# A convolution's eighth chunk ahead of the taps of the sixth and seventh, with all its taps on VectorE and GpSimd

## The chip, the cores and the metric

The kernel runs on one core of a Trainium2 chip. The metric is the device time of one execution in microseconds, as the median of several runs. TensorE, VectorE (DVE in the profile), ScalarE (ACT), GpSimd (POOL) and the DMA queues work side by side, each through its own instructions in order.

## What is computed

The program is a decoder trunk of two layers on 512 tokens of width 1024, in float32: a Conformer convolution module, then differential attention, each followed by a SwiGLU block and a gated embedding. The change lies in the convolution module of the first layer:

```python
a = x @ w_pw1 + b_pw1
u = a[..., :D_MODEL] * jax.nn.sigmoid(a[..., D_MODEL:])
u = lax.conv_general_dilated(u, dw_w[:, None, :], window_strides=(1,),
        padding=[(CONV_WIDTH - 1, 0)], ..., feature_group_count=D_MODEL) + dw_b
u = jax.nn.silu(layer_norm(u, ln_g, ln_b))
return u @ w_pw2 + b_pw2
```

The convolution is depthwise: each of the 1024 features has its own 31 taps over the tokens. The layer norm needs, for every token, the sum and the sum of squares over all 1024 features.

## The kernel before

Features lie on the 128 partitions and tokens along the free axis, so the 1024 features are eight chunks of 128x512, numbered 0 to 7 in the code; "the eighth chunk" is number 7. Large products run as three matmuls on high and low parts (`mm3`, L159 to L161); a weight tile is loaded by SyncE, rounded to its high part on ScalarE (L152) and its low part is taken on VectorE (L154).

The loop over `c` (L480 to L527) makes one chunk per turn. Two halves of 24 matmuls each (`half`) give the gate `pg` and the value `pa`; VectorE scales them (L503, L509), ScalarE takes the sigmoid (L504), and VectorE puts the chunk together (L521, or L513 for a phased chunk). The taps of chunk c-1 are in turn c.

There are two ways to do a chunk's 31 taps. The chunks 1, 3, 5 and 6 are *phased*: the chunk goes through DRAM into another layout (`phased_in`, buffers `pi` and `C1`), TensorE does all its taps as 36 matmuls with prepared matrices (`phased_taps`, L387; matrices loaded by SyncE at L367, L373 and L377 into the buffers `D0` to `D5` and `C5`), and the result goes back through DRAM: ScalarE copies it out of PSUM (L395) and starts the store (L397), SyncE loads it in four pieces (L400), and VectorE adds bias and shift (L405, called the shift below). The other chunks share their taps between engines. For chunk 7 TensorE does 8 taps with diagonal matrices (L343), ScalarE forms 7 products (L422, L425) that GpSimd adds (L426), and VectorE does 16 taps as one multiply-and-add each (L435, L438). VectorE then adds the three parts (L442, L444).

`moments` (L456) squares a finished chunk on ScalarE (L466) and adds square and chunk to running sums, on GpSimd for most chunks and on VectorE for chunk 6 (L471, L473). The last chunk is not added: TensorE sums over the partitions with matmuls by ones (L192), once for the running sums and once for the last chunk and its square. From these follow mean and variance (L565 to L567, L254, a power on GpSimd at L256), a row of factors (L575, L578), the normalised chunks (L589 to L594), and the second product (`linear`).

Between the taps and these sums stand five *factors*: `project` does a small product of the gated embedding ahead of time, six matmuls in a PSUM tile "mm", and ScalarE copies it out (L305). They are ordered behind the last tap on TensorE.

PSUM tiles come from pools: four "mm", two "sc" and two "tp" buffers, each one bank. A tile gets its buffer where the scheduler places its first use. The kernel's order on each engine is made by a scheduler that goes by estimated times and by the waits between instructions; `tc.issue_after(x)` keeps an instruction behind x.

Of the kernel before, what the change touches and what calls it, by code (L numbers as in the profile page):

```python
# [14 lines left out]
AF = mybir.ActivationFunctionType  # L15
ALU = mybir.AluOpType
# [4 lines left out]
P = 128  # L21
S = 512
# [4 lines left out]
KW = 31  # L27
# [20 lines left out]

SHIFT = 1
WARM = 9  # L50
ALONE = (7,)
CUTS = 2


PE_TAPS = (0, 0, 0, 0, 0, 0, 0, 8)
POOL_TAPS = (10, 0, 11, 0, 11, 0, 0, 7)


PHASED = (1, 3, 5, 6)
# [25 lines left out]
def trunk(ctx, tc, xT, pT, wts, diag, dww, vec, rel, onehot, lamv, out):  # L85
# [29 lines left out]
    def col(name, i=0):  # L115
        a, _ = VEC[name]
        return vt[:, a + i : a + i + 1]
# [181 lines left out]
    def project(ph, m, w, o, step=lambda: None):  # L299

        acc = mm()
        for k in range(2):
            last_product[0] = mm3(acc, wpart(w, 2 * (m % 4) + k), ph[k], k == 0, k == 1)
            step()
        last_copy[0] = A.copy(o, acc)  # L305
        return o

    last_copy = [None]
    y = []
    PAD = KW - 1  # L310
    ups = {}
    accs = {}
    last_tap = [None]
    last_out = [None]
    last_shift = [None]
    last_v_tap = [None]
    last_sum = [None]
    rb = None

# [6 lines left out]
    def wt(c, j):  # L326
        return dwt[:, c * KW + j : c * KW + j + 1]
# [64 lines left out]
    def phased_out(c):  # L392

        o = big()
        last_out[0] = A.copy(o, accs[c])  # L395
        d = dram.tile([P, S], F32, tag=f"po{c}", name=f"po{c}")
        nc.scalar.dma_start(d, o)  # L397
        both_ = sb([P, 2, S], f"B{c}", 1)
        for g in range(NPH):
            nc.sync.dma_start(  # L400
                both_[g * FG : (g + 1) * FG, 1].rearrange("p (r n) -> p r n", r=NPH),
                bass.AP(d.tensor, d.offset + g * P, [[S, FG], [FG * S, NPH], [1, P]]),
            )
        tok = "p (n r) -> p n r"
        last_shift[0] = V.scalar_tensor_tensor(  # L405
            both_[:, 0].rearrange(tok, r=NPH), both_[:, 1].rearrange("p (r n) -> p n r", r=NPH), col("dw_b", c),
            shrow.rearrange(tok, r=NPH), ALU.add, ALU.add,
        )
        y.append(both_[:, 0])

    def other_taps(c):
        if c in PHASED:
            return phased_out(c)
        up, acc = ups[c], accs[c]
        alone = c in ALONE
        tap = lambda j: up[:, j : j + S]
        a, b = PE_TAPS[c], PE_TAPS[c] + POOL_TAPS[c]
        pacc = wk()
        for j in range(a, b):
            if j == a:  # L420
                with tc.issue_after(last_out[0].ins) if alone else nullcontext():
                    A.activation(pacc, tap(j), AF.Identity, scale=wt(c, j), bias=col("dw_b", c))  # L422
            else:
                pr = sb([P, S], f"C{2 + j % 2}", 2)
                A.activation(pr, tap(j), AF.Copy, scale=wt(c, j))  # L425
                G.tensor_tensor(pacc, pacc, pr, ALU.add)  # L426
        yc = sb([P, 2, S], f"B{c}", 1)
        if c == 0:
            sums["acc"] = yc[:, 1]
        yc = yc[:, 0]  # L430
        sum_ = sc() if alone else acc
        if c == 0:
            V.tensor_scalar(sum_, tap(b), wt(c, b), None, ALU.mult)
        else:
            V.scalar_tensor_tensor(sum_, tap(b), wt(c, b), shrow, ALU.mult, ALU.add)  # L435
        for j in range(b + 1, KW):
            with tc.issue_after(last_shift[0].ins) if alone and j == KW - 4 else nullcontext():
                last_v_tap[0] = V.scalar_tensor_tensor(sum_, tap(j), wt(c, j), sum_, ALU.mult, ALU.add)  # L438
        if alone:
            moments(NC - 2)  # L440
        with tc.issue_after(last_sum[0].ins) if alone else nullcontext():
            V.tensor_tensor(yc, sum_, pacc, ALU.add)  # L442
        if alone:
            last_add[0] = V.tensor_tensor(yc, acc, yc, ALU.add)  # L444
        y.append(yc)

# [4 lines left out]
    macc = sb([P, S], "acc", 1)  # L451
    last_moment = [None]
    last_add = [None]
    last_factor = [None]

    def moments(c):  # L456
        if c == 0:
            t = tp()
            T.matmul(t, ones, y[0], start=True, stop=True)
            A.activation(shrow, t, AF.Copy, scale=-1.0 / P)  # L460
            V.scalar_tensor_tensor(y[0], t, -1.0 / P, y[0], ALU.mult, ALU.add)
            A.activation(sums["acc"], y[0], AF.Square)
            return
        sq = sums["sq"] = wk()
        with tc.issue_after(last_factor[0].ins) if c > NC - 3 else nullcontext():
            A.activation(sq, y[c], AF.Square)  # L466
        if c == NC - 1:
            return
        eng, at = (V, tc.issue_after(last_v_tap[0].ins)) if c == NC - 2 else (G, nullcontext())
        with at:  # L470
            last_sum[0] = eng.tensor_tensor(sums["acc"], sums["acc"], sq, ALU.add)  # L471
            if c > 1:
                eng.tensor_tensor(macc, y[1] if c == 2 else macc, y[c], ALU.add)  # L473

    def add_moments(a, b, first, last):

# [3 lines left out]
    for c in range(NC):  # L480
        wa, wg = pairs[c]
        if c == 0:
            pg = half(wg)
            pa = half(wa)
            norm.dg = diagonal(norm.columns_of_chunks())
            rb = norm.rows()
        if c + 1 < NC:
            pairs.append((weight(), weight())[::-1])
            pair_loads.append(loaded[0])
        if c == 0:  # L490
            dwt = sb([P, NC * KW], "C4", 2)
            nc.sync.dma_start(dwt, dww)
        if c == 1:
            ph = pfeatures(0, [(sb([P, S], t, 2, F32R), sb([P, S], t, 2, F32R)) for t in ("wth", "wtl")])
        if c > 0:
            pg = half(wg)
            if c - 1 not in PHASED:
                pe_taps(c - 1)
            pa = half(wa)
            if c - 1 in PHASED:  # L500
                pe_taps(c - 1)
        tg, ta = big(), big()
        V.tensor_tensor(tg, pg, rb, ALU.mult)  # L503
        gated = A.activation(tg, tg, AF.Sigmoid, bias=col("b_pw1", 8 + c))  # L504
        if c == NC - 1:

            with tc.issue_after(gated.ins):
                A.activation(sb([P, 8], "lam", 1), vt[:, :8], AF.Silu)
        V.tensor_tensor(ta, pa, rb, ALU.mult)  # L509
        if c in PHASED:  # L510
            up = big()
            phases, tok = "p (r n) -> p n r", "p (n r) -> p n r"
            V.scalar_tensor_tensor(  # L513
                up.rearrange(phases, r=NPH), ta.rearrange(tok, r=NPH), col("b_pw1", c),
                tg.rearrange(tok, r=NPH), ALU.add, ALU.mult,
            )
            phased_in(c, up)
        else:
            up = ups[c] = sb([P, S + PAD], "C0", 2)
            G.memset(up[:, :PAD], 0.0)  # L520
            V.scalar_tensor_tensor(up[:, PAD:], ta, col("b_pw1", c), tg, ALU.add, ALU.mult)  # L521
        if c > 0:
            other_taps(c - 1)
        if c == 1:
            moments(0)
        elif c > 3:
            moments(c - 3)  # L527
# [16 lines left out]
    moments(NC - 3)  # L544
    pe_taps(NC - 1)
    for m in range(5):
        factor(last_tap)
        if m == 1:
            last_factor[0] = last_copy[0]
    other_taps(NC - 1)  # L550
    moments(NC - 1)

    sums["cols"], sums["mean"], sums["mcols"] = tp(), tp(), sc()
    with tc.issue_after(last_product[0].ins):
        add_moments(macc, sums["acc"], True, False)
        add_moments(y[NC - 1], sums["sq"], False, True)
    factor(last_moment)

    with tc.issue_after(last_product[0].ins):
        T.matmul(sums["mean"], ones, macc, start=True, stop=False)  # L560
        last_product[0] = T.matmul(sums["mean"], ones, y[NC - 1], start=False, stop=True)


    vs = sb([P, P // 2], "v8", 2)[:, :8]
# [61 lines left out]
        V.scalar_tensor_tensor(h[m], acc, col("b_pw2", m), h[m], ALU.add, ALU.add)  # L626
        norm.chunk(m)

    linear(NC, z, add_conv, 3, split={0: (last_add[0], None), 1: (last_add[0], None), 2: (layer_v, None), 3: third}, home=("C5", 2))


    def ffn(norm, after):
# [510 lines left out]
```

## Time and profile before

| | us |
|---|---|
| median of 3 runs | 1277.39 (1276.99 to 1279.48) |
| profiled execution, its own time | 1276.96 |
| its span in the profile | 1275.0 |
| TensorE busy | 1264.7 |
| VectorE busy | 707.7 |
| ScalarE busy | 524.5 |
| GpSimd busy | 246.1 |

The span runs from the first instruction on any engine to the last; the execution's own time holds 1.96 us more around it. In the timeline a row has its start, its length, the engine, the line, the operation with its tiles, and behind brackets how long the engine had been idle and what ended that. Matmul rows overlap each other by some 0.16 us, so the pace of matmuls is read from start to start. The convolution's last part lies between 110 and 160 us of the span.

### The profile page before, as it was taken

What the parts mean: (1) busy time and instruction counts of PE and PEld (TensorE: products, weight loads), DVE (VectorE), ACT (ScalarE), POOL (GpSimd) and SP (SyncE); (2) the same over time, 40 slices, a digit from 0 to 9 for tenths busy, and PEclk for the clock granted to TensorE, in tenths of its full rate; (3) what the DMA queues carried; (4) which work ended last, traced back from release to release, by engine and by line L of the source; (5) the groups of instructions that cost most, each with busy time, mean ns of one, the idle gap of its engine ahead of it and who ended that gap; (6) DMA issues with size and microseconds to landing.
All of it is one profiled execution on the core that took longest, in us unless ns stands there. A gap on an engine that the chain in (4) does not pass through costs nothing.

```text
span 1275.0 us, 15493 instructions
## 1 busy us (share of the span) xinstructions
PE 1264.7 (99%) x5960; PEld 1050.7 (82%) x5960; DVE 707.7 (56%) x1042; ACT 524.5 (41%) x876; POOL 246.1 (19%) x223
## 2 busy tenths in 40 slices
PE   9999999999999999999999999999999999999998
PEld 8888788888888888888888888888888888888887
DVE  4997865543344434366777876646443444334545
ACT  5653454332222223254666877744231222123332
POOL 1654432000000000042346635141000000000120
PEclk9999999999999999999999999999999999999999
DMA  7655213333332222233432330133223333222231
GB/s 269 199 181 174 92 58 125 88 96 98 99 99 99 94 90 98 75 127 124 139 110 82 106 99 26 65 134 100 95 89 97 99 99 99 97 87 91 89 116 66
DMA packets 49142, 136.17 MB, mean 107 GB/s; under 512 B 5635, under 2 KB 10243, under 8 KB 49068
## 3 DMA queue, kind: packets, MB, share of 16 engines
q1 hardware_dynamic: 46944, 131.74, 31.6%
q10 hardware_dynamic: 2124, 3.43, 0.8%
q8 instruction: 47, 0.77, 0.2%
q14 instruction: 27, 0.22, 0.1%
HBM read 128.84 MB, written 6.31 MB: 106 GB/s over the span
## 4 chain that ended last, share of the span: by engine, by line
PE 87%; DVE 5%; DMA 3%; POOL 2%; issue 2%; ACT 1%; SPq 0%; POOLq 0%; DVEq 0%; ACTq 0%
PE mm L159 27%; PE mm L160 27%; PE mm L161 27%; DVE sc L438 2%; POOL wk L426 2%; PE mm L871 1%; DVE wlo L154 1%; DMA wraw<-in_wts 1%; DMA po<-big 1%; PE sc L839 1%; PE sc L838 1%; PE tp L858 1%; PE tp L792 1%; ACT whi L152 0%; ACT A L199 0%
## 5 line engine op out<-in xcount | busy, mean ns | idle before, releaser
L152 ACT CAST whi<-wraw 128x1024 fp32r<-128x1024 f32 (+2 forms) x209 | 213.2, 1026 | 551.3 <-PE mm L161 364.1
L159 PE MATMUL mm<-A,wlo 128*128 128x512 f32 (+1 forms) x1080 | 421.3, 390 | 0.6 <-ACT A L199 0.5
L160 PE MATMUL mm<-A,whi 128*128 128x512 f32 (+1 forms) x1080 | 419.3, 388 | 0.0
L161 PE MATMUL mm<-A,whi 128*128 128x512 f32 (+1 forms) x1080 | 416.0, 389 | 0.0
L154 DVE TENSOR_TENSOR wlo<-wraw,whi 128x1024 fp32r<-128x1024 f32 (+2 forms) x205 | 253.2, 1239 | 88.2 <-ACT whi L152 88.2
L159 PEld LDWEIGHTS mm<-A,wlo 128*128 128x128 f32 x1080 | 203.0, 188 | 43.7 <-issue 1.2
L160 PEld LDWEIGHTS mm<-A,whi 128*128 128x128 f32 x1080 | 203.0, 188 | 42.3 <-issue 1.2
L161 PEld LDWEIGHTS mm<-A,whi 128*128 128x128 f32 x1080 | 202.7, 188 | 41.4 <-issue 0.5
L223 POOL TENSOR_TENSOR acc<-acc,wk 128x512 f32<-128x512 f32 x35 | 57.9, 1653 | 772.3 <-issue 660.0
L159 PE MATMUL mm<-B,wlo 128*128 128x512 f32 x352 | 137.8, 391 | 0.0
L160 PE MATMUL mm<-B,whi 128*128 128x512 f32 x352 | 137.5, 390 | 0.0
L161 PE MATMUL mm<-B,whi 128*128 128x512 f32 x352 | 137.4, 390 | 0.0
L658 DVE TENSOR_TENSOR h<-mm,h 128x512 f32<-128x512 f32 x48 | 33.0, 691 | 123.3 <-PE mm L161 123.2
L650 DVE TENSOR_TENSOR big<-mm,rb 128x512 f32<-128x512 f32 x44 | 30.4, 691 | 126.4 <-PE mm L161 126.4
L648 DVE TENSOR_TENSOR big<-mm,rb 128x512 f32<-128x512 f32 x44 | 30.4, 691 | 99.9 <-PE mm L161 93.0
L161 PEld LDWEIGHTS mm<-B,whi 128*128 128x128 f32 x352 | 66.1, 188 | 14.5
L159 PEld LDWEIGHTS mm<-B,wlo 128*128 128x128 f32 x352 | 66.1, 188 | 14.3
L160 PEld LDWEIGHTS mm<-B,whi 128*128 128x128 f32 x352 | 66.1, 188 | 14.2
L159 PE MATMUL mm<-whi,A 128*128 128x512 f32 x192 | 76.5, 401 | 0.0
L161 PE MATMUL mm<-wlo,A 128*128 128x512 f32 x192 | 75.3, 398 | 0.0
L160 PE MATMUL mm<-whi,A 128*128 128x512 f32 x192 | 75.1, 393 | 0.0
L426 POOL TENSOR_TENSOR wk<-wk,C 128x512 f32<-128x512 f32 x35 | 51.9, 1483 | 24.4 <-ACT C L425 19.5
(225 smaller groups left out, 1378.0 us busy)
## 6 DMA issues: line engine op xcount, KB each, us to landing
wraw<-in_wts SPq DMA_DIRECT2D x193, 512.0 KB, 3.5
wraw<-in_wts SPq DMA_DIRECT2D x16, 384.0 KB, 2.9
D<-in_diag SPq DMA_DIRECT2D x22, 256.0 KB, 4.1
C<-in_diag SPq DMA_DIRECT2D x16, 256.0 KB, 5.0
h<-in_xT SPq DMA_DIRECT2D x8, 256.0 KB, 5.4
rest<-h SPq DMA_DIRECT2D x8, 256.0 KB, 3.0
bias<-scr ACTq DMA_DIRECT2D x8, 256.0 KB, 3.3
h<-rest SPq DMA_DIRECT2D x8, 256.0 KB, 2.7
```

Source lines behind the costliest of these rows:

```text
L152: A.copy(hi[:, cut], raw[:, cut])
L154: eng.tensor_tensor(lo[:, cut], raw[:, cut], f(hi[:, cut]), ALU.subtract)
L159: T.matmul(acc, al, bh, start=first, stop=False)
L160: T.matmul(acc, ah, bh, start=False, stop=False)
L161: return T.matmul(acc, ah, bl, start=False, stop=last)
L223: self.last = self.eng.tensor_tensor(self.acc, self.acc, sq, ALU.add)
L426: G.tensor_tensor(pacc, pacc, pr, ALU.add)
L438: last_v_tap[0] = V.scalar_tensor_tensor(sum_, tap(j), wt(c, j), sum_, ALU.mult, ALU.add)
L648: V.tensor_tensor(tg, pg, rb, ALU.mult)
L650: V.tensor_tensor(tu, pu, rb, ALU.mult)
L658: V.tensor_tensor(h[m], acc, h[m], ALU.add)
L792: T.transpose(t[:, i * P : (i + 1) * P], q[:, i * P : (i + 1) * P], ident)
```

## The change

Chunk 7's taps leave TensorE: GpSimd (with ScalarE) takes 10 of the 31, VectorE 21. Its accumulator on VectorE is the tile `accs[7]`, which `pe_taps` takes from the "mm" pool and which TensorE used before. The turn c = 6 does no taps, and in turn 7 both halves of chunk 7 come ahead of the taps of chunks 5 and 6. `phased_out` is split: storing and loading stay in it, the shift is `phased_shift`. The shift of chunk 5 is put between chunk 7's taps, behind tap 21. The running sums take in chunk 7 (on VectorE), and the chunk that is left for last is chunk 6.

```diff
-PE_TAPS = (0, 0, 0, 0, 0, 0, 0, 8)
-POOL_TAPS = (10, 0, 11, 0, 11, 0, 0, 7)
+PE_TAPS = (0, 0, 0, 0, 0, 0, 0, 0)
+POOL_TAPS = (10, 0, 11, 0, 11, 0, 0, 10)
...
-        sum_ = sc() if alone else acc
         if c == 0:
-            V.tensor_scalar(sum_, tap(b), wt(c, b), None, ALU.mult)
+            V.tensor_scalar(acc, tap(b), wt(c, b), None, ALU.mult)
         else:
-            V.scalar_tensor_tensor(sum_, tap(b), wt(c, b), shrow, ALU.mult, ALU.add)
+            V.scalar_tensor_tensor(acc, tap(b), wt(c, b), shrow, ALU.mult, ALU.add)
         for j in range(b + 1, KW):
-            with tc.issue_after(last_shift[0].ins) if alone and j == KW - 4 else nullcontext():
-                last_v_tap[0] = V.scalar_tensor_tensor(sum_, tap(j), wt(c, j), sum_, ALU.mult, ALU.add)
-        if alone:
-            moments(NC - 2)
-        with tc.issue_after(last_sum[0].ins) if alone else nullcontext():
-            V.tensor_tensor(yc, sum_, pacc, ALU.add)
-        if alone:
-            last_add[0] = V.tensor_tensor(yc, acc, yc, ALU.add)
-        y.append(yc)
+            r = V.scalar_tensor_tensor(acc, tap(j), wt(c, j), acc, ALU.mult, ALU.add)
+            if between and j == KW - 10:
+                with tc.issue_after(r.ins):
+                    between()
+        last_add[0] = V.tensor_tensor(yc, acc, pacc, ALU.add)
...
             pg = half(wg)
-            if c - 1 not in PHASED:
-                pe_taps(c - 1)
             pa = half(wa)
-            if c - 1 in PHASED:
-                pe_taps(c - 1)
+            for k in ([c - 1], [], [c - 2, c - 1])[max(0, c - NC + 3)]:
+                pe_taps(k)
...
-    moments(NC - 3)
+    copies = []
+    phased_out(NC - 3)
+    phased_out(NC - 2)
     pe_taps(NC - 1)
     for m in range(5):
         factor(last_tap)
-        if m == 1:
-            last_factor[0] = last_copy[0]
-    other_taps(NC - 1)
+    other_taps(NC - 1, lambda: phased_shift(NC - 3))
+    moments(NC - 3)
     moments(NC - 1)
+    with tc.issue_after(last_sum[0].ins):
+        last_add[0] = phased_shift(NC - 2)
+    moments(NC - 2)
...
-        add_moments(y[NC - 1], sums["sq"], False, True)
+        add_moments(y[NC - 2], sums["sq"], False, True)
```

In `moments` the squares of chunks 6 and 7 are ordered behind the copies of the fifth and fourth factor, and the square of chunk 6 is the one that is not added to the running sum. The third weight of `linear` is rounded behind that square.

More of the change, by code (lines that the diff above doesn't have):

```diff
@@ L50 @@
 WARM = 9
-ALONE = (7,)
 CUTS = 2
-PE_TAPS = (0, 0, 0, 0, 0, 0, 0, 8)
-POOL_TAPS = (10, 0, 11, 0, 11, 0, 0, 7)
+PE_TAPS = (0, 0, 0, 0, 0, 0, 0, 0)
+POOL_TAPS = (10, 0, 11, 0, 11, 0, 0, 10)
 PHASED = (1, 3, 5, 6)
@@ L308, in trunk @@
     last_copy = [None]
-    y = []
+    y = [None] * NC
     PAD = KW - 1
@@ L313, in trunk @@
     last_tap = [None]
-    last_out = [None]
-    last_shift = [None]
-    last_v_tap = [None]
     last_sum = [None]
@@ L394, in phased_out @@
         o = big()
-        last_out[0] = A.copy(o, accs[c])
+        A.copy(o, accs[c])
         d = dram.tile([P, S], F32, tag=f"po{c}", name=f"po{c}")
         nc.scalar.dma_start(d, o)
-        both_ = sb([P, 2, S], f"B{c}", 1)
+        both_ = y[c] = sb([P, 2, S], f"B{c}", 1)
         for g in range(NPH):
@@ L403, in phased_out, with phased_shift @@
             )
-        tok = "p (n r) -> p n r"
-        last_shift[0] = V.scalar_tensor_tensor(
+    def phased_shift(c):
+        both_, tok = y[c], "p (n r) -> p n r"
+        y[c] = both_[:, 0]
+        return V.scalar_tensor_tensor(
             both_[:, 0].rearrange(tok, r=NPH), both_[:, 1].rearrange("p (r n) -> p n r", r=NPH), col("dw_b", c),
@@ L408, in phased_out, with other_taps @@
         )
[L409 to L413, printed above, removed]
+    def other_taps(c, between=None):
         up, acc = ups[c], accs[c]
-        alone = c in ALONE
         tap = lambda j: up[:, j : j + S]
-        a, b = PE_TAPS[c], PE_TAPS[c] + POOL_TAPS[c]
+        b = POOL_TAPS[c]
         pacc = wk()
[L419 to L422, printed above, removed]
+        for j in range(b):
+            if j == 0:
+                A.activation(pacc, tap(j), AF.Identity, scale=wt(c, j), bias=col("dw_b", c))
             else:
@@ L429, in other_taps @@
             sums["acc"] = yc[:, 1]
-        yc = yc[:, 0]
-        sum_ = sc() if alone else acc
+        yc = y[c] = yc[:, 0]
         if c == 0:
-            V.tensor_scalar(sum_, tap(b), wt(c, b), None, ALU.mult)
+            V.tensor_scalar(acc, tap(b), wt(c, b), None, ALU.mult)
         else:
-            V.scalar_tensor_tensor(sum_, tap(b), wt(c, b), shrow, ALU.mult, ALU.add)
+            V.scalar_tensor_tensor(acc, tap(b), wt(c, b), shrow, ALU.mult, ALU.add)
         for j in range(b + 1, KW):
-            with tc.issue_after(last_shift[0].ins) if alone and j == KW - 4 else nullcontext():
-                last_v_tap[0] = V.scalar_tensor_tensor(sum_, tap(j), wt(c, j), sum_, ALU.mult, ALU.add)
-        if alone:
-            moments(NC - 2)
-        with tc.issue_after(last_sum[0].ins) if alone else nullcontext():
-            V.tensor_tensor(yc, sum_, pacc, ALU.add)
-        if alone:
-            last_add[0] = V.tensor_tensor(yc, acc, yc, ALU.add)
-        y.append(yc)
+            r = V.scalar_tensor_tensor(acc, tap(j), wt(c, j), acc, ALU.mult, ALU.add)
[3 more added lines that the diff above has]
+        last_add[0] = V.tensor_tensor(yc, acc, pacc, ALU.add)
     shrow = sb([P, S], "shrow", 1)
@@ L453, in trunk @@
     last_add = [None]
-    last_factor = [None]
+    last_square = [None]
     def moments(c):
@@ L464, in moments @@
         sq = sums["sq"] = wk()
-        with tc.issue_after(last_factor[0].ins) if c > NC - 3 else nullcontext():
-            A.activation(sq, y[c], AF.Square)
-        if c == NC - 1:
+        with tc.issue_after(copies[10 - c].ins) if c >= NC - 2 else nullcontext():
+            last_square[0] = A.activation(sq, y[c], AF.Square)
+        if c == NC - 2:
             return
-        eng, at = (V, tc.issue_after(last_v_tap[0].ins)) if c == NC - 2 else (G, nullcontext())
+        eng, at = (V, tc.issue_after(last_add[0].ins)) if c == NC - 1 else (G, nullcontext())
         with at:
-            last_sum[0] = eng.tensor_tensor(sums["acc"], sums["acc"], sq, ALU.add)
             if c > 1:
                 eng.tensor_tensor(macc, y[1] if c == 2 else macc, y[c], ALU.add)
+            last_sum[0] = eng.tensor_tensor(sums["acc"], sums["acc"], sq, ALU.add)
     def add_moments(a, b, first, last):
@@ L521, in trunk @@
             V.scalar_tensor_tensor(up[:, PAD:], ta, col("b_pw1", c), tg, ALU.add, ALU.mult)
-        if c > 0:
-            other_taps(c - 1)
+        if 0 < c < NC - 2:
+            (phased_out if c - 1 in PHASED else other_taps)(c - 1)
+            if c - 1 in PHASED:
+                phased_shift(c - 1)
         if c == 1:
@@ L542, in factor @@
             pp.append(project(ph, m, pw[m // 4], o))
-    moments(NC - 3)
+        copies.append(last_copy[0])
+    copies = []
+    phased_out(NC - 3)
+    phased_out(NC - 2)
     pe_taps(NC - 1)
@@ L560, in trunk @@
         T.matmul(sums["mean"], ones, macc, start=True, stop=False)
-        last_product[0] = T.matmul(sums["mean"], ones, y[NC - 1], start=False, stop=True)
+        last_product[0] = T.matmul(sums["mean"], ones, y[NC - 2], start=False, stop=True)
     vs = sb([P, P // 2], "v8", 2)[:, :8]
@@ L627, in add_conv @@
         norm.chunk(m)
-    linear(NC, z, add_conv, 3, split={0: (last_add[0], None), 1: (last_add[0], None), 2: (layer_v, None), 3: third}, home=("C5", 2))
+    linear(NC, z, add_conv, 3, split={0: (last_add[0], None), 1: (last_add[0], None), 2: (layer_v, last_square[0]), 3: third}, home=("C5", 2))
     def ffn(norm, after):
```

## The prediction, made before the changed kernel was run

> **What bounds the kernel now.** I read the page first, then TensorE by stretches, then VectorE's and ScalarE's rows in time order. The page:
>
> ```profile
> PE 1264.7 (99%) x5960; PEld 1050.7 (82%) x5960; DVE 707.7 (56%) x1042; ACT 524.5 (41%) x876; POOL 246.1 (19%) x223
> ```
>
> TensorE is busy 99% of the span, so an edit gains only what it takes off TensorE, and loses what it makes TensorE wait. The stretch that changes, cut where one kind of matmul gives way to the next (columns: stretch, its length, PE busy and count, granted clock, DMA share, GB/s):
>
> ```profile
> 111.40:119.84 8.44, 8.05 (x73) 1.00 0.55 188
> 119.84:127.65 7.81, 7.81 (x37) 1.00 0.90 296
> 127.65:135.69 8.04, 8.04 (x74) 1.00 0.41 112
> 135.69:142.16 6.47, 6.47 (x19) 1.00 0.40 141
> 142.16:149.39 7.23, 7.23 (x33) 1.00 0.00 1
> 149.39:153.30 3.91, 3.91 (x34) 1.00 0.00 0
> ```
>
> In order: the sixth chunk's taps (after 0.39 us without work), the rest of the eighth chunk's projection, the seventh's taps, the eighth's eight taps on TensorE, five factors, the layer norm's column sums. Beside them VectorE (start, length, what):
>
> ```profile
> 115.84 3.92 DVE L438 SCALAR_TENSOR_TENSOR sc<-C,C,sc 128x512 f32<-128x512 f32 x5
> ...
> 122.41 0.69 DVE L503 TENSOR_TENSOR big<-mm,rb 128x512 f32<-128x512 f32 x1 [1.86 <-PE mm L161]
> 126.33 0.15 DVE L730 TENSOR_SCALAR lam<-vec 128x1 f32<-128x1 f32 x1 [3.23 <-ACT lam L508]
> ...
> 131.00 1.12 DVE L405 SCALAR_TENSOR_TENSOR B<-B,vec,shrow 128x512 f32<-128x512 f32 x1 [4.45 <-DMA B<-po]
> 132.04 0.68 DVE L509 TENSOR_TENSOR big<-mm,rb 128x512 f32<-128x512 f32 x1
> 132.75 1.34 DVE L521 SCALAR_TENSOR_TENSOR C<-big,vec,big 128x512 f32<-128x512 f32 x1
> 134.13 1.66 DVE L435 SCALAR_TENSOR_TENSOR sc<-C,C,shrow 128x512 f32<-128x512 f32 x1
> 135.82 8.67 DVE L438 SCALAR_TENSOR_TENSOR sc<-C,C,sc 128x512 f32<-128x512 f32 x11
> 144.40 1.16 DVE L405 SCALAR_TENSOR_TENSOR B<-B,vec,shrow 128x512 f32<-128x512 f32 x1
> 145.49 3.12 DVE L438 SCALAR_TENSOR_TENSOR sc<-C,C,sc 128x512 f32<-128x512 f32 x4
> 148.51 0.68 DVE L473 TENSOR_TENSOR acc<-acc,B 128x512 f32<-128x512 f32 x1
> 149.11 0.68 DVE L471 TENSOR_TENSOR B<-B,wk 128x512 f32<-128x512 f32 x1
> 149.71 0.68 DVE L442 TENSOR_TENSOR B<-sc,wk 128x512 f32<-128x512 f32 x1
> 150.50 0.69 DVE L444 TENSOR_TENSOR B<-mm,B 128x512 f32<-128x512 f32 x1
> 151.11 2.35 DVE L154 TENSOR_TENSOR wlo<-wraw,whi 128x1024 fp32r<-128x1024 f32 x2
> ...
> 153.84 0.16 DVE L567 SCALAR_TENSOR_TENSOR v<-tp,v 128x4 f32<-128x4 f32 x1
> ```
>
> The eighth chunk's output is complete at 150.50 + 0.69 = 151.19, and TensorE's last sums start with it: today the two engines arrive together. From here on the layer norm is a chain, so whatever moves the last chunk's output moves the rest of the kernel as one block. Two numbers are compared below: the last output (151.19) and L567, which waits for the last column sums (153.84).
>
> **The change, part by part.** *TensorE.* The eighth chunk's projection comes ahead of the sixth's taps, its eight taps leave. From 111.40: projection 7.81, taps 8.05 (its projection is in SBUF by then, and the 0.39 us wait for VectorE goes), taps 8.04: the factors start at 135.30, not 142.16, 6.86 us earlier (6.47 and 0.39). The seventh chunk's tap matrices reuse the sixth's buffers, whose last reads now end only as the seventh's begin; each still has about 4 us from release to use, so I count 0, and up to 1 us late.
>
> *The accumulator: the term that decides.* VectorE now sums the eighth chunk's taps in the tile that TensorE used, one of the four "mm" tiles in PSUM, where before it summed in an "sc" tile of its own. In the program as built from the changed kernel, that tile is given the bank of the **second factor's product**: the first tap on VectorE (the new L428) waits for ScalarE's copy of that factor (L304, today L305), and VectorE's later work is queued in order behind it. So the projection was moved forward for taps that cannot start until the factors run. ScalarE's copies and its square of the last output:
>
> ```profile
> 144.14 0.59 ACT L305 COPY D<-mm 128x512 f32<-128x512 f32 x1 [2.81 <-PE mm L161]
> 145.50 0.59 ACT L305 COPY D<-mm 128x512 f32<-128x512 f32 x1 [0.78 <-PE mm L161]
> ...
> 151.23 0.63 ACT L466 ACTIVATE wk<-B 128x512 f32<-128x512 f32 x1 [1.47 <-DVE B L444]
> ```
>
> The second copy ends at 146.09, 3.93 us after the factors' start; so at 139.2 afterwards. Today the first tap starts at 134.13.
>
> *VectorE's chain from 139.2.* One tap more ahead of the shift, and nine in place of four behind it: 21 taps for 16. What the first tap costs depends on GpSimd:
>
> ```profile
> 73.23 0.74 DVE L435 SCALAR_TENSOR_TENSOR sc<-C,C,shrow 128x512 f32<-128x512 f32 x1
> 137.95 8.72 POOL L426 TENSOR_TENSOR wk<-wk,C 128x512 f32<-128x512 f32 x6 [2.72 <-ACT wk L422]
> ```
>
> It took 1.66 at 134.13 and 0.74 at 73.23; the bounds are these two. GpSimd's nine adds (six today, 1.45 each) take 13.1 us from about 126, once the eighth chunk and its first products are there, and end at about 139, as the tap starts: I take 0.77 with the step to the next. [...]
>
> Then: 0.77 → 139.97; eleven taps as at 135.82, to the next start 8.58 → 148.55; the sixth chunk's shift, 1.09 to the next start → 149.64; nine taps of 0.79 (8.67 for eleven) = 7.1 → 156.75; one add with GpSimd's part, 0.79 as from 149.71 to 150.50 (today two adds, the second is gone) → 157.54; the sum of outputs at 157.54, done at 158.2; the sum of squares waits for ScalarE's square of the eighth chunk (157.5 + 0.63) → 158.15; the seventh's shift 0.60 later and 1.12 long → **159.87**. Its data landed long before (today 144.40 at the latest, for taps that end 0.39 later). Against 151.19 this is **+8.7 us**. TensorE's 6.86 us are hidden entirely: they bring the factors' end to 142.53, and TensorE then waits until 158.2. ScalarE's three more products, GpSimd's three more adds and two diagonal loads of 256 KB less lie beside that wait and cost nothing.
>
> *TensorE after a wait of 15.7 us.* No row shows one: its longest idle here is 1.19 us. The nearest are the kernel's first matmuls, which also follow idleness, against equal ones in mid-kernel:
>
> ```profile
> 1.51 4.21 PE L134 MATMUL tp<-ones,ident 128*128 128x128 f32 x18 [1.51 <-POOL ident masks.py:199]
> 5.37 0.77 PE L159 MATMUL mm<-A,wlo 128*128 128x512 f32 x1
> 5.95 0.60 PE L160 MATMUL mm<-A,whi 128*128 128x512 f32 x1
> 6.37 1.07 PE L192 MATMUL tp<-ones,wk 128*128 128x128 f32 x8
> ...
> 149.39 1.05 PE L192 MATMUL sc<-ones,acc 128*128 128x128 f32 x8
> ```
>
> Eighteen passes took 4.21 us, 0.23 each; eight take 0.89 to the next group at 150.28 or about 0.11 each; full pace came near 6.0, 4.5 us after the first. The granted clock reads 1.00 for both, so it does not show this. Bounds: nothing is lost, or all four groups of column sums run at 1.87 instead of about 0.95. Nearest row, same kind of matmul: half pace for 4.5 us. Sums of outputs from 158.25 to 160.1, of squares to 162.0, the seventh chunk's (ready at 159.9) to 163.3 with the pace rising at 162.75, its squares to 164.3; L567's successor at about 164.4, **+10.5 us** against 153.84. At full pace throughout, the four end at 162.0, but VectorE's two weight splits (2.27) last to 162.14 and the two short steps ahead of it 0.46: 162.65, +8.8. At half pace throughout, 165.7 and 165.9: +12.0. [...]
>
> **Sum.** The profiled execution took 1276.96 us (span 1275.0 and 1.96 around it); the median of the three runs, 1277.39, is 0.43 above. 1276.96 + 8.7 for the last output + 1.8 for the cold restart = **1287.5 us**. Past L567 the order is the same, with the same distances.
>
> **Rivals.**
> *A, the wait does not bind* (the bank is free in time, and the change does what it says). The tap could start when the eighth chunk is ready: three of the five taps at 115.84 done by 118.2, then its gate multiplication; the small constants ended 4.1 us after that one's start (122.41 to 126.5), so 122.3, then one add, 0.6, 0.68 and up to 1.34 → 124.9. Then the sixth chunk's shift binds. Its taps end at 127.3, and from taps' end to shift today took 8.7 us (135.69 to 144.40) and 11.2 us (119.84 to 131.00): 136.0 to 138.5. From that start to the last output are 11.3 us in my chain: 147.3 to 149.8, 1.4 to 3.9 us earlier than 151.19, so **1274.4 us**, up to 1276 if a short wait of TensorE slows its restart. It decides at one point: last output = first tap + 20.7, so the change is not slower if the first tap starts by 130.5. Against it: the tap's wait stands in the built program and ends at 139.2. For it: only that I misread which instruction the wait counts to.
>
> *B, the wait binds and TensorE keeps its pace:* +8.7 and 0.1, **1285.8 us**. For it: the granted clock never falls in this trace. Against: the first matmuls' half pace.
>
> *C, half pace throughout, and a late tap matrix or a long first tap (0.9):* +12.0 and 0.9, **1289.9 us**. For it: tap matrices are loaded closer to their use. Against: GpSimd ends first by my count.
>
> **How the numbers follow.** My forecast has 0.58, B 0.2, C 0.15, A 0.07. The range 1284.6 to 1290.4 holds the first three with 0.5 to 1 us for the profiled execution against a median; A lies outside. A measurement of this kernel tells about 0.2% (2.6 us) from no change: below 1274.8 is faster, above 1279.9 slower. A is split: 0.03 faster, 0.04 the same; 0.93 slower.
>
> **What would show it.** Right: in the changed profile VectorE stands idle from about 124 until ScalarE's second factor copy at about 139, and the wait row of its first tap names that copy; the last shift ends near 160; TensorE idles some 15 us behind the fifth factor and its next column sums take nearly 2 us for eight passes; past the layer norm all rows keep their distances. Wrong: the first tap before 130, a shift that ends near 149, column sums at 0.1 us a pass straight after the idle time, or gaps in TensorE among the seventh chunk's taps.

## The result, and the profile after

The changed kernel took **1289.08 us** (median of 4 runs, 1288.46 to 1289.69). The kernel before took 1278.37 in the runs beside it (4 runs, 1276.99 to 1279.48). The ratio is 1.0083, 95% interval 1.007 to 1.0096: about 10.7 us slower. The profiled execution took 1289.4, its span is 1287.4. Lines of the changed kernel stand up to twelve lower than before; the first tap on VectorE is L428, the taps L430, the shift L404, ScalarE's factor copies L304, the column sums L191, and L567's successor is L562.

From the page, busy time by engine:

```profile
PE 1261.3 (98%) x5944; PEld 1049.3 (82%) x5944; DVE 709.9 (55%) x1046; ACT 526.8 (41%) x879; POOL 249.9 (19%) x226
```

TensorE has 3.4 us less to do than before, and the span is 12.4 us longer. VectorE in order of time shows where they went (start, length, what, idle time ahead and what ended it):

```profile
122.31 0.68 DVE L497 TENSOR_TENSOR big<-mm,rb 128x512 f32<-128x512 f32 x1
123.03 1.33 DVE L509 SCALAR_TENSOR_TENSOR C<-big,vec,big 128x512 f32<-128x512 f32 x1
139.09 0.76 DVE L428 SCALAR_TENSOR_TENSOR mm<-C,C,shrow 128x512 f32<-128x512 f32 x1 [14.73 <-ACT D L304]
139.88 8.67 DVE L430 SCALAR_TENSOR_TENSOR mm<-C,C,mm 128x512 f32<-128x512 f32 x11
148.46 1.09 DVE L404 SCALAR_TENSOR_TENSOR B<-B,vec,shrow 128x512 f32<-128x512 f32 x1
149.46 7.08 DVE L430 SCALAR_TENSOR_TENSOR mm<-C,C,mm 128x512 f32<-128x512 f32 x9
...
157.44 0.69 DVE L461 TENSOR_TENSOR acc<-acc,B 128x512 f32<-128x512 f32 x1
158.10 0.69 DVE L462 TENSOR_TENSOR B<-B,wk 128x512 f32<-128x512 f32 x1
158.72 1.10 DVE L404 SCALAR_TENSOR_TENSOR B<-B,vec,shrow 128x512 f32<-128x512 f32 x1
...
164.20 0.16 DVE L562 SCALAR_TENSOR_TENSOR v<-tp,v 128x4 f32<-128x4 f32 x1 [0.54 <-PE tp L191]
```

The eighth chunk is ready at 124.36, and the first tap, which needs nothing else but its accumulator, waits 14.73 us. ScalarE's rows say which copy it waits for:

```profile
137.11 0.59 ACT L304 COPY D<-mm 128x512 f32<-128x512 f32 x1 [0.79 <-PE mm L160]
138.47 0.59 ACT L304 COPY D<-mm 128x512 f32<-128x512 f32 x1 [0.77 <-PE mm L160]
```

The second of them ends at 139.06, 0.03 ahead of the tap. GpSimd's share of the taps was done before that, at 138.07:

```profile
125.96 12.11 POOL L420 TENSOR_TENSOR wk<-wk,C 128x512 f32<-128x512 f32 x9 [0.46 <-ACT C L419]
```

TensorE pays for the first tap's wait later. Its column sums in order of time:

```profile
158.19 2.08 PE L191 MATMUL sc<-ones,acc 128*128 128x128 f32 x8 [15.69 <-DVE acc L461]
160.06 1.92 PE L191 MATMUL tp<-ones,B 128*128 128x128 f32 x8
161.77 1.50 PE L191 MATMUL sc<-ones,B 128*128 128x128 f32 x8
163.11 1.06 PE L191 MATMUL tp<-ones,wk 128*128 128x128 f32 x8
```

The idle time has moved from VectorE to TensorE: 15.69 us, ended by the running sum, and the first two groups of eight passes take twice as long as the last. The changed kernel by stretches (stretch, length, busy time and count of PE, PEld, DVE, ACT and POOL, then the granted clock, the DMA share and GB/s) shows why:

```profile
142.50:145.00 2.50, 0.01 (x1) 0.00 (x0) 2.39 (x4) 0.58 (x1) 0.00 (x0) 1.00 0.09 26
145.00:150.00 5.00, 0.00 (x0) 0.00 (x0) 4.86 (x7) 0.42 (x1) 0.37 (x1) 0.56 0.00 2
150.00:158.00 8.00, 0.00 (x0) 0.00 (x0) 7.51 (x11) 0.84 (x2) 2.12 (x2) 0.50 0.00 0
158.00:162.00 4.00, 3.81 (x18) 3.81 (x19) 4.00 (x5) 1.57 (x3) 0.00 (x0) 0.50 0.00 0
162.00:164.00 2.00, 2.00 (x17) 2.00 (x16) 0.41 (x3) 0.00 (x0) 0.00 (x0) 0.83 0.96 276
```

The granted clock goes to 0.50 some 3.1 us after the last factor (at 145.63) and comes back to 1.00 only at 162.70. L562 stands at 164.20 where L567 stood at 153.84: +10.36. That is nearly the whole difference of the medians, 10.7. The two profiled spans differ by 2 us more, in small steps over the attention and SwiGLU stretches that the change does not touch. No run shows where these steps come from; the profiled execution of before was one of its shortest.

### The profile page after: what moved, and what is told of

It is laid out like the page before. It is cut to its first block, busy times and chain, and to the rows that moved or that the text cites. A ratio compares the mean times of both kernels' runs of the same rounds, so it can differ in the third digit from the quotient of the medians.

```text
span 1287.4 us, 15469 instructions
## 1 busy us (share of the span) xinstructions
PE 1261.3 (98%) x5944; PEld 1049.3 (82%) x5944; DVE 709.9 (55%) x1046; ACT 526.8 (41%) x879; POOL 249.9 (19%) x226
## 4 chain that ended last, share of the span: by engine, by line
PE 97%; DVE 2%; DMA 0%; ACT 0%; issue 0%; POOL 0%; SPq 0%; DVEq 0%
PE mm L158 29%; PE mm L159 29%; PE mm L160 29%; PE sc L383 2%; PE mm L866 1%; DVE mm L430 1%; PE tp L191 1%; PE sc L834 1%; PE sc L833 1%; PE tp L853 1%; PE mm L383 1%; PE tp L787 1%; DMA wraw<-in_wts 0%; PE tp L270 0%; PE sc L191 0%; PE tp L896 0%
## 5 line engine op out<-in xcount | busy, mean ns | idle before, releaser
L420 POOL TENSOR_TENSOR wk<-wk,C 128x512 f32<-128x512 f32 x38 | 55.0, 1448 | 22.3 <-ACT C L419 19.9
```

## The experiments

**Theory:** the time is lost because VectorE's accumulator shares a PSUM bank with the second factor; the order of the work itself is sound. **Rival:** the order is at fault (21 taps in a row, the late shifts), and the bank only decides when the chain starts. Line numbers shift by a few between the kernels; "the 'sc' version" is the one of the first experiment. Ratios are to the kernel before on the same chip.

### The accumulator in an "sc" buffer

```diff
-        acc = accs[c] = sc() if c < NC - 2 else mm()
+        acc = accs[c] = mm() if c == NC - 2 else sc()
```

> The changed kernel with one tile moved: the eighth chunk's accumulator on VectorE comes from the two "sc" tiles in PSUM, not from the four "mm" tiles that the factors use. Theory (the first tap waits for the second factor's bank): the first tap starts at about 124 instead of 139, the last output is ready near 146, the time falls some 5 us below the kernel before, to about 1273.5 us. Rival (21 taps on VectorE in place of 16, and the sums' new end, cost the time by themselves): the last output stays past 151 and the time stays at 1280 us or above.

Measured: 1275.4 us (8 runs, 1273.8 to 1277.09; before 1279.29), ratio 0.997 (0.996 to 0.998); some 1273.5 was expected. VectorE and then TensorE of this version, in order of time:

```profile
122.40 1.34 DVE L509 SCALAR_TENSOR_TENSOR C<-big,vec,big 128x512 f32<-128x512 f32 x1
123.78 1.65 DVE L428 SCALAR_TENSOR_TENSOR sc<-C,C,shrow 128x512 f32<-128x512 f32 x1
125.47 11.05 DVE L430 SCALAR_TENSOR_TENSOR sc<-C,C,sc 128x512 f32<-128x512 f32 x14
136.42 1.95 DVE L404 SCALAR_TENSOR_TENSOR B<-B,vec,shrow 128x512 f32<-128x512 f32 x1
...
145.17 1.13 DVE L404 SCALAR_TENSOR_TENSOR B<-B,vec,shrow 128x512 f32<-128x512 f32 x1
...
148.95 0.16 DVE L562 SCALAR_TENSOR_TENSOR v<-tp,v 128x4 f32<-128x4 f32 x1
```

```profile
144.64 1.16 PE L191 MATMUL sc<-ones,acc 128*128 128x128 f32 x8 [2.06 <-DVE acc L461]
```

The first tap starts as soon as its chunk is there. Everything behind it is 15.25 us earlier than in the changed kernel (164.20 to 148.95), and 4.9 earlier than before the change. The medians differ by less, 3.9. In this execution, the shortest of the eight, TensorE waits 2.06 us in place of 15.69 and keeps its pace; the mean clock of the others says that most of them do not (last experiments). One buffer decides the sign of the change.

### TensorE kept busy through the wait

The changed kernel with 62 matmuls added whose results nothing uses:

```diff
+    for k in range(62):
+        with tc.issue_after(last_product[0].ins):
+            last_product[0] = T.matmul(sums["mean"], pw[1][0][:, 0:P], ph[0][0], start=True, stop=True)
```

> The changed kernel with 62 idle matmuls of 128x512 between the fifth factor and the column sums, written into a tile that is overwritten afterwards: TensorE stays busy for about 14 us of its 15.7 us wait. Theory (the restart at half pace is a term of its own, 1.7 us): column sums at 0.11 us a pass, the granted clock stays at 1.0, the steps behind the last sums come 1.7 us earlier than in the changed kernel, about 1287.4 us. Rival (the column sums wait for VectorE and ScalarE, not for the clock): no change from 1289 us. The first tap's wait stays as it is in both.

Measured: 1287.39 us (5 runs, 1287.08 to 1287.8), ratio 1.0066 (1.0052 to 1.0079). TensorE and VectorE of it:

```profile
142.11 14.21 PE L551 MATMUL tp<-wth,whi 128*128 128x512 f32 x62
158.02 1.16 PE L191 MATMUL sc<-ones,acc 128*128 128x128 f32 x8 [1.69 <-DVE acc L461]
159.01 1.06 PE L191 MATMUL tp<-ones,B 128*128 128x128 f32 x8
```

```profile
158.54 1.11 DVE L404 SCALAR_TENSOR_TENSOR B<-B,vec,shrow 128x512 f32<-128x512 f32 x1
...
162.30 0.16 DVE L565 SCALAR_TENSOR_TENSOR v<-tp,v 128x4 f32<-128x4 f32 x1
```

The last shift is where it was (158.54, 158.72), the column sums run at full pace, and the last short step comes 1.9 us earlier, 0.18 of it because the shift is that much earlier. So the restart at half pace is worth 1.7 us in the rows. The two medians also differ by 1.7; they come from separate sets of runs, and by their ratios the gain is some 2.2.

### The order alone, undone

The version with the "sc" accumulator, with the sixth's taps back between the seventh's and the eighth's projection:

```diff
-            for k in ([c - 1], [], [c - 2, c - 1])[max(0, c - NC + 3)]:
-                pe_taps(k)
+            pe_taps(c - 1)
```

> The accumulator in an "sc" tile as in the first experiment, and the order of the projection and the taps put back as it was before the change (the sixth chunk's taps inside the eighth's projection): what is left is the taps' move off TensorE and the new end of the sums. Theory (bringing the projection forward is worth what VectorE gains by starting early): first tap near 130, last output near 151.5, TensorE waits some 7 us behind the factors and restarts slowly, about 2 us above the kernel before, 1280.5 us. Rival (the order matters little once the accumulator is free): the same time as the first experiment within 1 us.

Measured: 1279.61 us (11 runs, 1279.13 to 1280.27), ratio 1.0009 (1.0 to 1.0018). VectorE and TensorE:

```profile
129.21 0.76 DVE L428 SCALAR_TENSOR_TENSOR sc<-C,C,shrow 128x512 f32<-128x512 f32 x1
...
154.18 0.16 DVE L561 SCALAR_TENSOR_TENSOR v<-tp,v 128x4 f32<-128x4 f32 x1 [0.53 <-PE tp L191]
```

```profile
148.31 2.08 PE L191 MATMUL sc<-ones,acc 128*128 128x128 f32 x8 [5.80 <-DVE acc L461]
```

The first tap is 5.43 us later than with the new order, the end 5.23. The time is near the 1280.5 that was expected. So the new order is worth about 5 us in this stretch (4.2 in the medians, 1279.61 to 1275.4 on one chip), some of it again a restart at half pace behind a wait of 5.80 us. The rival falls.

### The sums' end alone, undone

The "sc" version in which the running sums end with the seventh chunk again: its shift and its two additions stand ahead of the eighth chunk's last addition, and the column sums left for last are the eighth's. From the edit, in which `other_taps` runs `seventh` behind its last tap:

```diff
-    other_taps(NC - 1, lambda: phased_shift(NC - 3))
-    moments(NC - 3)
...
+    def seventh():
+        last_shift[0] = phased_shift(NC - 2)
+        moments(NC - 2)
+
+    other_taps(NC - 1, sixth, seventh)
     moments(NC - 1)
-    with tc.issue_after(last_sum[0].ins):
-        last_add[0] = phased_shift(NC - 2)
-    moments(NC - 2)
...
-        add_moments(y[NC - 2], sums["sq"], False, True)
+        add_moments(y[NC - 1], sums["sq"], False, True)
```

> The version of e1_acc_sc with the third part of the change undone: the running sums end with the eighth chunk's predecessor again (the seventh chunk's shift and its two additions stand on VectorE ahead of the eighth chunk's final addition), and the last column sums are the eighth chunk's. VectorE has the same instructions in another order. My theory is that ending with the seventh chunk is worth something only because that chunk goes through DRAM: in e1_acc_sc its load was issued over 141.52 to 143.25 us and takes 2.1 us to land, so about 145.3, while the taps end at 143.0. Here the shift would wait for it, 145.3 to 146.4; the two additions to 147.8, the eighth chunk's output at 148.5; TensorE, which is through with its factors at 142.5, stands until 147.1, close to 5 us, and so runs its column sums slowly (as in e3_old_order after 5.8 us): the last short step on the means at about 153.5 instead of 148.95, +4.5 us, 1280 us. At full pace after that wait: 150.5, +1.5 us, 1277. The rival is that the order of the sums is only bookkeeping (same instructions on VectorE, data there in time): +0.5 us, 1276. The row of the seventh chunk's shift decides: it either waits for the load to 145 or later, or starts at 143.

Measured: 1278.76 us (11 runs, 1278.04 to 1280.32; before 1278.44), ratio 1.0002 (0.9993 to 1.001). VectorE and TensorE:

```profile
138.10 4.69 DVE L430 SCALAR_TENSOR_TENSOR sc<-C,C,sc 128x512 f32<-128x512 f32 x6
144.71 1.09 DVE L404 SCALAR_TENSOR_TENSOR B<-B,vec,shrow 128x512 f32<-128x512 f32 x1 [1.93 <-DMA B<-po]
...
153.08 0.16 DVE L572 SCALAR_TENSOR_TENSOR v<-tp,v 128x4 f32<-128x4 f32 x1 [0.54 <-PE tp L191]
```

```profile
146.65 2.07 PE L191 MATMUL sc<-ones,acc 128*128 128x128 f32 x8 [4.27 <-DVE acc L466]
```

The shift waits for its load, as expected, TensorE stands 4.27 us and restarts at half pace: the end is 4.1 us later than with the new sums (4.5 expected). The last output, 147.18 + 0.68, is 1.6 us later than in the "sc" version (146.30); the rest of the 4.1 is the slow column sums. So the rival, that the order is only bookkeeping, falls. What the third part buys is that VectorE's final addition and two additions (143.10 to 145.17 in the "sc" version) cover that transfer, and that TensorE's wait stays short.

### ScalarE's square moved, and taps moved to GpSimd

The "sc" version with ScalarE's square of the sixth chunk behind its copy of the seventh's taps:

```diff
-        with tc.issue_after(copies[10 - c].ins) if c >= NC - 2 else nullcontext():
+        at = copies[10 - c] if c >= NC - 2 else last_out[0] if c == NC - 3 else None
+        with tc.issue_after(at.ins) if at is not None else nullcontext():
```

> The version of e1_acc_sc with one edit: ScalarE's square of the sixth chunk, which stood waiting for VectorE's shift until 138.41 with the copy of the seventh chunk's taps behind it (138.94), is kept behind that copy. The copy then comes at about 135.2, the seventh chunk is stored and loaded 3.5 us earlier, and TensorE's 0.43 us wait for that bank goes. My theory is that this is worth nothing by itself, since VectorE's chain sets the end (the last shift began at 145.17 straight after the additions, not after a transfer): 1275.4 us, with TensorE's idle time ahead of the column sums grown from 2.06 to about 2.5. The rival, that ScalarE's copies and the transfer set the end: up to 1 us faster, 1274.4.

Measured: 1275.73 us (11 runs, 1274.1 to 1276.87), ratio 0.9973 (0.9964 to 0.9982): no gain, as the theory has it. Two things were not foreseen. ScalarE's rows:

```profile
135.60 0.59 ACT L391 COPY big<-mm 128x512 f32<-128x512 f32 x1 [2.10 <-PE mm L383]
139.09 0.63 ACT L457 ACTIVATE wk<-B 128x512 f32<-128x512 f32 x1 [2.90 <-DVE B L404]
139.15 0.33 ACTq L393 DMA_DIRECT2D po<-big  x1
```

The copy came at 135.60, but its store stands in the same queue behind the square and was issued at 139.15, so the transfer did not move. The rival, that the transfer sets the end, was therefore not put to the test here; against it speaks that the last shift's row in the "sc" version (145.17) has no wait. And TensorE, by stretches and in order of time:

```profile
145.00:145.30 0.30, 0.00 (x0) 0.00 (x0) 0.30 (x2) 0.30 (x2) 0.00 (x0) 0.96 0.00 0
145.30:146.00 0.70, 0.68 (x3) 0.68 (x4) 0.70 (x2) 0.31 (x1) 0.00 (x0) 0.50 0.00 0
```

```profile
145.32 2.07 PE L191 MATMUL sc<-ones,acc 128*128 128x128 f32 x8 [2.94 <-DVE acc L463]
```

The clock fell 2.9 us after the last factor's matmul, just as this wait of 2.94 us ended. In the profiled "sc" version, with a wait of 2.06 us, it did not fall.

With that edit and two more of the eighth chunk's taps on ScalarE and GpSimd:

```diff
-POOL_TAPS = (10, 0, 11, 0, 11, 0, 0, 10)
+POOL_TAPS = (10, 0, 11, 0, 11, 0, 0, 12)
...
-            if between and j == KW - 10:
+            if between and j == KW - 8:
```

> The version of e1_acc_sc with two edits: ScalarE's square of the sixth chunk is kept behind its copy of the seventh chunk's taps (as in e6_square_later), and two more of the eighth chunk's taps go from VectorE to ScalarE and GpSimd (12 instead of 10), the sixth chunk's shift staying two taps earlier in the count so that it starts at the same time. My theory is that the stretch is now set by VectorE's chain, first tap 123.8 to the sum of outputs: two taps of 0.79 less bring the outputs' sum from 143.90 to 142.3 and the last shift from 145.17 to 143.6, TensorE's idle time ahead of the column sums falls from 2.06 to about 0.5 to 0.9, and the last short step comes 1.3 to 1.6 us earlier: 1274.0 us. GpSimd's eleven additions end near 140.5 and its two additions of the sixth chunk at 142.8 to 143.1, which may hold the second running sum by 0.1 to 0.3. The rival: GpSimd or the seventh chunk's transfer sets the end instead, and nothing is gained (1275.4) or up to 1 us is lost (1276.4).

Measured: 1275.94 us (9 runs, 1274.83 to 1277.27), ratio 0.998 (0.997 to 0.9989). The expected gain did not come, the rival did. GpSimd and VectorE:

```profile
140.88 1.30 POOL L420 TENSOR_TENSOR wk<-wk,C 128x512 f32<-128x512 f32 x1
142.13 1.28 POOL L464 TENSOR_TENSOR B<-B,wk 128x512 f32<-128x512 f32 x1
143.35 1.28 POOL L420 TENSOR_TENSOR wk<-wk,C 128x512 f32<-128x512 f32 x1
```

```profile
144.67 0.69 DVE L434 TENSOR_TENSOR B<-sc,wk 128x512 f32<-128x512 f32 x1 [2.08 <-POOL wk L420]
```

The scheduler put the sixth chunk's two additions (L464 is the second) between GpSimd's last taps, and VectorE waited 2.08 us for the last of them. TensorE, after its own wait, shows something else:

```profile
146.14 1.45 PE L191 MATMUL sc<-ones,acc 128*128 128x128 f32 x8 [3.56 <-DVE acc L463]
147.38 1.92 PE L191 MATMUL tp<-ones,B 128*128 128x128 f32 x8
149.09 1.63 PE L191 MATMUL sc<-ones,B 128*128 128x128 f32 x8
150.55 1.06 PE L191 MATMUL tp<-ones,wk 128*128 128x128 f32 x8
```

This wait, 3.56 us, is longer than the 2.94 above, and yet the column sums did not begin at half pace: the first group took 1.45 us, where it took 1.16 in the "sc" version and 2.07 with the square moved. By an estimate the pace fell at some 146.9, 0.7 us after work had resumed, and came back at some 150.3. It is worked out from the time from start to start: the first group took 0.99 us with TensorE kept busy (158.02 to 159.01) and 1.87 in the changed kernel (158.19 to 160.06), the next 0.90 (159.01 to 159.91) and 1.71 (160.06 to 161.77).

### Keeping the clock, and a version with both mended

Three kernels on one chip: the "sc" version with nine unused matmuls behind the factors; the "sc" version again; and one with eleven taps on GpSimd, its additions of the sixth chunk behind them, the seventh's store ahead of the square, and six unused matmuls.

```diff
+    for k in range(9):
+        with tc.issue_after(last_product[0].ins):
+            last_product[0] = T.matmul(sums["mean"], pw[1][0][:, 0:P], ph[0][0], start=True, stop=True)
```

> The version of e1_acc_sc with nine matmuls of 128x512 added that compute nothing used, behind the fifth factor's last matmul: at 0.227 us each they fill the 2.06 us in which TensorE waits for the running sum. My theory, from e1_acc_sc and e6_square_later: a wait of 2 to 3 us sometimes halves TensorE's clock and sometimes not (the profiled e1_acc_sc with 2.06 us kept its pace, the profiled e6_square_later with 2.94 us ran two groups of column sums in 2.07 and 1.78 us; the eight executions of e1_acc_sc fall in two heaps, spans 1272.0 to 1272.5 at a mean granted clock of 0.999 to 1.000 and 1273.3 to 1274.3 at 0.998). With TensorE busy every execution should lie in the first heap: mean clock 0.999 or more, median about 1274.0 us, 1.4 below e1_acc_sc. The rival: the heaps have another cause (the kernel before spreads over 1274.2 to 1278.3 at an unchanged clock), and the median stays at 1275.4 with the same spread.

> The kernel of e1_acc_sc unchanged, on the same chip as the two others, to compare the heaps of its executions with theirs. Theory: two heaps, about 1.7 us apart, the higher one at a mean clock of 0.998 or less and the lower at 0.999 or more; median about 1275.4 us.

```diff
-POOL_TAPS = (10, 0, 11, 0, 11, 0, 0, 10)
+POOL_TAPS = (10, 0, 11, 0, 11, 0, 0, 11)
...
-        nc.scalar.dma_start(d, o)
+        last_out[0] = nc.scalar.dma_start(d, o)
...
-            if between and j == KW - 10:
+            if between and j == KW - 9:
...
-        eng, at = (V, tc.issue_after(last_add[0].ins)) if c == NC - 1 else (G, nullcontext())
+        eng, at = (V, tc.issue_after(last_add[0].ins)) if c == NC - 1 else (G, tc.issue_after(last_pool[0].ins) if c == NC - 3 else nullcontext())
...
+    for k in range(6):
+        with tc.issue_after(last_product[0].ins):
+            last_product[0] = T.matmul(sums["mean"], pw[1][0][:, 0:P], ph[0][0], start=True, stop=True)
```

> The version of e1_acc_sc with four edits towards a faster one: eleven of the eighth chunk's taps on ScalarE and GpSimd (VectorE 20), GpSimd's two additions of the sixth chunk behind its last tap (in e5_pool12_square_later they stood between the taps, and VectorE waited 2.08 us for GpSimd's part), ScalarE's copy and store of the seventh chunk ahead of its square of the sixth, and six unused matmuls that keep TensorE busy to the column sums. Theory: VectorE's chain is one tap of 0.79 us shorter, the running sum comes at 143.1 to 143.8, all else follows, and the clock stays full: 0.8 us below e7_acc_sc_busy, about 1273.2 us. The rival: GpSimd, one addition of 1.3 us longer, or the transfer of the seventh chunk sets the end: no gain over e7_acc_sc_busy or up to 1 us lost, 1274.0 to 1275.0.

| version (before 1279.3, 9 runs) | median us | ratio | spans of the 5 runs at mean granted clock |
|---|---|---|---|
| "sc" again | 1275.35 | 0.9964 (0.9952 to 0.9977) | 1272.3, 1272.4 at 0.999 to 1.000; 1273.6, 1273.8, 1274.0 at 0.998 |
| with nine matmuls | 1274.74 | 0.9961 (0.9948 to 0.9975) | 1272.2 to 1273.2, all at 0.999 to 1.000 |
| with eleven taps on GpSimd | 1273.63 | 0.9955 (0.9942 to 0.9967) | 1271.6 to 1272.4, all at 1.000 |

The clock did what the theory says: with TensorE busy no execution has the lower mean clock, and without it three of five have, 1.5 us longer. The spans did so in part only. All five were expected among the short ones, 1272.0 to 1272.5, but four of the five with nine matmuls lie between the two heaps, at 1272.7 to 1273.2, so the clock is not the only source of spread. The gain in the median was 0.6 us, not 1.4; the intervals overlap, so its size stays open. The third version, VectorE and TensorE:

```profile
124.76 1.65 DVE L428 SCALAR_TENSOR_TENSOR sc<-C,C,shrow 128x512 f32<-128x512 f32 x1
...
149.08 0.16 DVE L568 SCALAR_TENSOR_TENSOR v<-tp,v 128x4 f32<-128x4 f32 x1
```

```profile
144.79 1.16 PE L191 MATMUL sc<-ones,acc 128*128 128x128 f32 x8 [0.55 <-DVE acc L464]
```

From the first tap to the last short step it takes 24.32 us, against 25.17 in the "sc" version (123.78 to 148.95): 0.85 for one tap less. Its median is the lowest of all versions measured, 0.45% below the kernel before (1273.2 us was expected). It is 1.1 us below the version with nine matmuls, but the intervals of the two ratios overlap.

## Why the prediction was right

- **The wait on the second factor's copy** was the term that decided, and it held: first tap at 139.09 (139.2 predicted). The "sc" version shows that it is the cause and not a companion. Why the scheduler gave the tile that bank no run tests.
- **VectorE's chain** came out row by row: first tap 0.76 (0.77 with the step), shift at 148.46 (148.55), add at 156.65 (156.75), last shift done at 159.82 (159.87). GpSimd ended at 138.07, ahead of the tap, as assumed; where it was not ahead, in the "sc" version, the first tap took 1.65, the other bound. The prediction had looked at GpSimd's tap products alone: beside the slow first tap of before (134.13) ran an addition for the running sums, which began at 133.50 and took 1.73 (L471).
- **TensorE's 6.86 us** were hidden entirely: they became part of a wait of 15.69 us.
- **The cold restart** was put at 1.8 us from the kernel's first matmuls; with TensorE kept busy it measured 1.7 in the rows. One sentence beside it was too weak: that the granted clock does not show it. At the kernel's start it does not (1.00 from 0 to 8 us); in the changed kernel it reads 0.50 from 145.63 to 162.70. That full pace came 4.5 us after the restart at 158.19, as at the kernel's start, is in part luck: over the other versions it took 3.4 to 5.4.
- **The sum:** L562 at 164.20 against 164.4, +10.36 against +10.5. The median came out 1.6 us above 1287.5, because the sum was made on an execution of 1276.96 where the median of before is 1278.37 by all its runs; the difference of the medians is 10.7. By the median alone rival C (1289.9) would be nearer; the rows tell them apart, since neither a late matrix, nor a long first tap, nor half pace to the end is in them. That past the layer norm all rows keep their distances held only to within the 2 us of the result section.
- **Rival A** (the wait does not bind) is what the "sc" version makes true: last shift done at 146.30, where 147.3 to 149.8 was worked out, and 1275.4 us where 1274.4 was. Its shift came at 136.42, inside the 136.0 to 138.5 given, and was longer (1.95, GpSimd still adding). Unlike in A it was not what bound: VectorE did 15 taps ahead of it instead of 12, and its row has no wait. A's other step held: in the run with the old order the first tap started at 129.21, ahead of the 130.5 given, the last output came 20.7 us later, and the time was that of before.
- **The tap matrices** cost nothing that shows: the factors start at 135.45, against 135.30.

## What to carry to other kernels

When an instruction is moved ahead, look at what its buffer waits for as well as its data: in this pool four buffers go round among many tiles, and an accumulator whose user was moved ended up behind a tile that is used later. The row of the first instruction of the moved block, with its idle time and releaser, tells this at once. And look at what stands between a copy and its store on the engine that issues both: ScalarE's copy, brought forward to 135.60, did not bring its store forward (issued at 139.15), since the square that waited for VectorE until 139.09 stood between them.

## What the runs showed of the hardware

- In the stretches read by window in this part of the kernel, TensorE's granted clock was 1.00 or 0.50, and in between only where a window holds a change from one to the other. The time at 0.50 was 17.07 us in the changed kernel (145.63 to 162.70), some 6.8 with the old order (145.7 to 152.5) and with the eighth chunk last (145.2 to 152.0), and 3.4 with the square moved (145.28 to 148.68): close to five, two, two and one times 3.41. The clock fell 2.8 to 3.2 us after the last matmul in these four profiles and came back 3.4 to 5.4 us after work resumed. With twelve taps on GpSimd the estimate above gives 3.4 us of half pace, 4.3 us after the last matmul.
- So the length of a wait does not decide alone. Waits of 2.94, 4.27, 5.80 and 15.69 us ended at half pace, one of 3.56 did not (first group 1.45 us, the fall by the estimate 0.7 us later), and waits of 2.06 and 2.02 (the two profiles of the "sc" version) had no fall. One kernel can do both: of the 13 executions of the "sc" version five have a mean clock of 0.999 or more (spans 1272.0 to 1272.5), eight 0.998 (1273.3 to 1274.3). What sets the two apart was not shown: no execution of the slower heap was traced.
- Two of VectorE's instructions were longer in the "sc" version than in the changed kernel. GpSimd was adding there when the first tap began at 123.78 (L462, 123.15 to 124.87) and when the shift began at 136.42 (nine additions from 125.34 to 137.50): 1.65 and 1.95 us, against 0.76 and 1.09 in the changed kernel, where GpSimd was idle. In the kernel before it was the other way round: the shift at 144.40 kept its 1.16 us, and GpSimd's addition that began at 144.73 took 1.95 us, with a median of 1.28. Why one of the two is longer was not shown. GpSimd's additions there, grouped by line (shortest, median and longest in ns, first and last start):

```profile
L426 POOL TENSOR_TENSOR wk<-wk,C x6: 1267/1280/1945, 137.9 to 144.7; 128x512 f32<-128x512 f32 x6
```

- The taps that keep their sum in PSUM took 0.79 us each in both cases (11.05 for 14 in the "sc" version, 8.67 for 11 in the changed kernel). So in the "sc" version the two instructions with both inputs in SBUF, the first tap and the shift, were longer beside GpSimd's additions, and the other taps were not.
- The kernel before spreads over 1274.2 to 1278.3 us of span (18 executions on one chip) at a mean clock of 0.999 to 1.000. No run here shows why.
